# High and low parts of the weight units at addresses that differ from unit to unit, in a hybrid decoder block on one core

## The chip, the core and the metric

The kernel runs on one core of a Trainium2 chip. The metric is the device time of one execution in microseconds. Matrix products are done by TensorE (PE; its loads of the stationary operand are PEld), elementwise work by VectorE (DVE) and ScalarE (ACT), and GpSimd (POOL) and SyncE (SP) mainly start transfers. Each of the 128 partitions of the on-chip memory has its own row of bytes; an address below is a byte offset in that row.

## What is computed

One layer of a decoder block on 256 tokens of width 2048, in fp32. The reference, cut to what matters:

```python
def reference(x, p, w_in, ..., w_gate, w_up, conv_w, conv_b, w_down, ..., w_ple_gate, w_ple_proj):
    mix = token_mixers(x, w_in[i], ..., w_branch_gla[i], w_branch_fox[i], w_out[i])
    x = layer_norm(ALPHA * x + mix, ln1_g[i], ln1_b[i])
    ffn = conv_gated_mlp(x, w_gate[i], w_up[i], conv_w[i], conv_b[i], w_down[i])
    x = layer_norm(ALPHA * x + ffn, ln2_g[i], ln2_b[i])
    x = x + jax.nn.sigmoid(x @ w_ple_gate[i]) * (p[i] @ w_ple_proj[i])

def token_mixers(x, w_in, ...):
    proj = x @ w_in            # q, k, v, gates of two branches, and two merge gates
...
    merged = jax.nn.sigmoid(ma) * y_gla + jax.nn.sigmoid(mb) * y_fox
    return merged @ w_out

def conv_gated_mlp(x, w_gate, w_up, conv_w, conv_b, w_down):
    g = causal_dwconv(x @ w_gate, conv_w, conv_b)
    h = jax.nn.gelu(g) * (x @ w_up)
    return h @ w_down
```

## The kernel before, in words

Nearly all of the work is products of 256 tokens with large weight matrices, in fp32 precision out of a faster matmul format (fp32r). Each operand is split into a high part (its rounding to that format, a copy on ScalarE) and a low part (the operand less its high part, a subtraction on VectorE), and a product is high x high + high x low + low x high.

The weights come as 284 units of 128 x 2048 fp32 (wu, 1 MB each), in one order that the host lays out. unit() hands out the next one and lets prep() run up to three units ahead. prep() loads each half of a unit into a ring of five raw tiles (1024 elements of a partition), makes its high part with copy() (line 121) in a tile of the pool rhi and its low part (line 241) in a tile of the pool rlo. Both pools have six slots. prep_s() does the same for units whose products go by a Strassen scheme; there the block differences are split, in split() (lines 121 and 215).

The units are used in two ways:

- As the stationary operand: w_unit() (lines 307 and 309) and w_phase() (lines 322 and 326), units 0 to 31 (q and k of both branches) and 136 to 223 (gate and up). For each of 16 blocks of 128 input rows one matmul of 512 columns has a 128 x 128 block of the high part as weights (the activation's high and low part stream past it), and one of 256 columns has the same block of the low part.
- As the moving operand: x_mm() (line 353), s_half() (line 841, and 909 in the last half) and q_unit() (line 979), all other units. There 512 columns of a part stream past a 128 x 128 block of the activation.

Where things lie: the built program puts the slots of rhi at 25088, 29184 and so on, 4096 bytes apart, and those of rlo at 49664, 54272 and so on, 4608 apart; all of these are multiples of 256. lo_tile() starts the low part 64 bytes (LO_SHIFT = 16 elements) into its slot where the unit is stationary, and at its start where it is moving (UA lists those units). The activations (xT, x1T, x2T, hC, mS, mC, oT and others) start at multiples of 256, and matmuls use blocks of them at steps of 512 or more. A few tiles lie otherwise: vh, which holds the high part of a head's values for line 1084 as a moving operand, is at 221632, and vl of the first 128 tokens at 225728, both 192 past a multiple of 256 (vl of the other 128 tokens is at 206592 or 208640, multiples of 256). The sums xS of two of the Strassen pairs, stationary in line 841, use the same two places. gp (line 1425) is written from its third element on, 8 bytes past its start; up, of the same shape, from its start.

The order of each engine's instructions is set by the program and the scheduler of the tile framework from what each instruction reads and writes; SP's order is the program's.

Of the kernel before, what the change touches and what calls it, by code (L numbers as in the profile page):

```python
# [10 lines left out]
F32R = mybir.dt.float32r  # L11
# [8 lines left out]
P = 128  # L20
# [15 lines left out]
GAPS = (96, 64, 80)  # L36


LO_SHIFT = 16
UA = (range(32, 136), range(224, 284))  # L40
P_STAT = 5000
P_LN1 = (4000, 2000)
P_LN2 = (4000, 1000)
# [35 lines left out]
def tile_block(ctx: ExitStack, tc: tile.TileContext, wu, wfv, wpp, xT_in, x_in, pT_in, wlr,  # L79
# [11 lines left out]
    rhi = ctx.enter_context(tc.tile_pool(name="rhi", bufs=6))  # L91
    rlo = ctx.enter_context(tc.tile_pool(name="rlo", bufs=6))
# [12 lines left out]
    def s8(shape, dt=F32, name=None):  # L105
        return big.tile(shape, dt, tag="S8", name=name)

    def t1(name):
        return sm.tile([P, 256], F32, tag="t1", bufs=6, name=name)
# [10 lines left out]
    def copy(o, i, scale=1.0):  # L120
        return nc.scalar.activation(o, i, AF.Copy, bias=0.0, scale=scale)  # L121
# [29 lines left out]
    hS = {}  # L151

    def lo_tile(u, name):
        o = 0 if any(u in r for r in UA) else LO_SHIFT
        return rlo.tile([P, 1152], F32R, tag="lo", name=f"lo{name}")[:, o:o + 1024]

    def differences(r0, r1, h, pinned=False):
        b12, b11, b22, b21 = r0[:, 0:512], r0[:, 512:1024], r1[:, 0:512], r1[:, 512:1024]
        sub = lambda o, a, b: nc.vector.tensor_tensor(o, a, b, ALU.subtract)  # L159
        if h == 0:  # L160
            i = sub(b11, b12, b11)
            if pinned:
                tc.keep_in_program_order(i)
            sub(b12, b12, b22)
        else:
            sub(b22, b22, b11)
            sub(b21, b21, b22)
# [17 lines left out]
    def prep_s(u):  # L185


        r0, r1 = [ring.tile([P, 1024], F32, tag="raw", bufs=5, name=f"raw{u}_{h}")
                  for h in range(2)]
        b12, b11, b22, b21 = r0[:, 0:512], r0[:, 512:1024], r1[:, 0:512], r1[:, 512:1024]  # L190
        rt = (r0, r1)
        if u in parked:
            nc.sync.dma_start(b11, wu[u, :, 512:1024])
            nc.sync.dma_start(r1, wu[u, :, 1024:2048])
            w = s8([P, 2048], name=f"td{u}")
            nc.sync.dma_start(w, td[parked[u]])
            rt = (w[:, 0:1024], w[:, 1024:2048])
        else:
            for h, r in enumerate((r0, r1)):
                nc.sync.dma_start(r, wu[u, :, h * 1024:(h + 1) * 1024])  # L200
        if dn0 <= u < dn0 + NF:
            nh = (u - dn0) // (NF // 2)
            pair = DN_ORDER[nh][(u - dn0) % (NF // 2)]
            i = DN_S[0].index(pair)
            if i % 2 == 0:
                two = s8([P, 8, 256], F32R, name=f"hS{nh}_{pair}")
                nc.sync.dma_start(two.bitcast(F32), sd[i // 2].rearrange(
                    "p (i n) -> p i n", i=8))
                hS[nh, pair], hS[nh, DN_S[0][i + 1]] = two[:, 0:4], two[:, 4:8]

        def split(src, name, e=slice(0, 1024)):
            hi = rhi.tile([P, 1024], F32R, tag="hi", name=f"hi{u}_{name}")[:, e]
            lo = lo_tile(u, f"{u}_{name}")[:, e]
            copy(hi, src)
            nc.vector.tensor_tensor(lo, src, hi.bitcast(F32), ALU.subtract)  # L215
            return [(hi[:, o:o + 512], lo[:, o:o + 512]) for o in range(0, src.shape[1], 512)]

        x11, = split(b11, "b11", slice(512, 1024))
        x22, x21 = split(r1, "b2")
        if u not in parked:  # L220
            differences(r0, r1, 0)
        t3, t1_ = split(rt[0], "t13")
        if u not in parked:
            differences(r0, r1, 1)
        t2_, t4 = split(rt[1], "t24")
        ready[u] = [x11, x21, x22, t1_, t3, t2_, t4]

    def prep(pinned=False):
        u = n_prep[0]
        n_prep[0] += 1  # L230
        if u in s_units:
            prep_s(u)
            return
        his, los = [], []
        for h in range(2):
            raw = ring.tile([P, 1024], F32, tag="raw", bufs=5, name=f"raw{u}_{h}")
            nc.sync.dma_start(raw, wu[u, :, h * 1024:(h + 1) * 1024])
            hi = rhi.tile([P, 1024], F32R, tag="hi", name=f"hi{u}_{h}")
            copy(hi, raw)
            lo = lo_tile(u, f"{u}_{h}")  # L240
            i = nc.vector.tensor_tensor(lo, raw, hi.bitcast(F32), ALU.subtract)  # L241
            if pinned:
                tc.keep_in_program_order(i)
            his.append(hi)
            los.append(lo)
        ready[u] = (his, los)


    def unit(ahead=3):
        u = n_used[0]  # L250
        n_used[0] += 1
        while n_prep[0] < min(NU, u + ahead):
            prep()
        return ready.pop(u)
# [203 lines left out]
    for u in range(8):  # L458
        hi, lo = fvu[u]
        for j in range(2):  # L460
# [8 lines left out]
            for t, i, c in seq:  # L469
                o, n = fch[c]  # L470
# [14 lines left out]
        elif u == 4:  # L485
            load_consts()
    prep()
    prep()
    wraw = s8([GROWS, 1024], name="wraw")
    nc.gpsimd.memset(wraw, 0.0)  # L490
# [161 lines left out]
    for n in range(16):  # L652
        h, j = n // 2, n % 2
        hi, lo = unit()
# [114 lines left out]
    for n in range(16):  # L769
        nm, dst, sc = (("q", gq, 1.0 / 16.0), ("k", gk, 1.0))[n // 2 % 2]  # L770
        h, c = n // 4, n % 2
        hi, lo = unit()
# [647 lines left out]
    for n in range(NF):  # L1420
# [18 lines left out]
        u = t1("up")  # L1439
# [4 lines left out]
        if pair in DN_S[0]:  # L1444
            if j == 0:
                yp = t2("yp").rearrange("p (k t) -> p k t", t=S)
            h = yp[:, j, :]
        else:
            h = y
# [4 lines left out]
        if pair in DN_S[0] and j == 1:  # L1454
            v = s_sums(yp)
            for i in range(2):
# [5 lines left out]
                o = k % 2 * 1024 + 512 * i  # L1462
# [295 lines left out]
```

## Time and profile before

| | |
|---|---|
| time, median of 2 runs | 1645.2 us (1645.02 to 1645.38) |
| span of the profiled execution | 1645.0 us |
| granted TensorE clock | 1.000 of full |
| TensorE busy | 1638.4 us (100%), 8422 matmuls |
| weight loads busy | 1404.3 us (85%) |
| VectorE busy | 1356.0 us (82%) |
| ScalarE busy | 910.3 us (55%) |
| moved from and to HBM | 417.53 MB read, 58.73 MB written, 290 GB/s |

The profiled execution took as long as the runs, so its span stands for them. TensorE's matmuls overlap each other in the records: the duration of one (389 ns for 512 columns) is longer than the step from its start to the next one's start, and that step is what adds up to the span. In rows in order of time the first number is a start in us from the span's start, the second the duration. In a group's row the three durations are minimum, median and maximum in ns. In a row by windows stand the window, its length, busy time with the count of instructions, the granted clock, and the DMA engines' share and rate.

### The profile page before, as it was taken

What the parts mean: (1) busy time and instruction counts of PE and PEld (TensorE: products, weight loads), DVE (VectorE), ACT (ScalarE), POOL (GpSimd) and SP (SyncE); (2) the same over time, 40 slices, a digit from 0 to 9 for tenths busy, and PEclk for the clock granted to TensorE, in tenths of its full rate; (3) what the DMA queues carried; (4) which work ended last, traced back from release to release, by engine and by line L of the source; (5) the groups of instructions that cost most, each with busy time, mean ns of one, the idle gap of its engine ahead of it and who ended that gap; (6) DMA issues with size and microseconds to landing.
All of it is one profiled execution on the core that took longest, in us unless ns stands there. A gap on an engine that the chain in (4) does not pass through costs nothing.

```text
span 1645.0 us, 23490 instructions
## 1 busy us (share of the span) xinstructions
PE 1638.4 (100%) x8422; PEld 1404.3 (85%) x8422; DVE 1356.0 (82%) x1964; ACT 910.3 (55%) x1277; POOL 92.7 (6%) x244
## 2 busy tenths in 40 slices
PE   9999999999999999999999999999999999999998
PEld 9988888888888888887898888888888888888887
DVE  7687899788989867778987888887887778988887
ACT  6655555456666654446574445555455456566554
POOL 0000000000000000000010111110111000000000
PEclk9999999999999999999999999999999999999999
DMA  8799799878888768889855898888766679899574
GB/s 324 281 371 341 290 383 356 294 258 309 306 333 307 252 207 303 305 335 364 296 190 194 315 338 320 308 306 304 279 239 217 210 260 336 305 343 348 177 258 157
DMA packets 114838, 477.81 MB, mean 290 GB/s; under 512 B 13032, under 2 KB 14320, under 8 KB 95136
## 3 DMA queue, kind: packets, MB, share of 16 engines
q1 hardware_dynamic: 105216, 417.57, 70.8%
q0 software_dynamic: 9504, 58.73, 8.9%
q8 instruction: 66, 1.08, 0.2%
q14 instruction: 52, 0.43, 0.1%
HBM read 417.53 MB, written 58.73 MB: 290 GB/s over the span
## 4 chain that ended last, share of the span: by engine, by line
PE 97%; DMA 1%; DVE 1%; ACT 0%; issue 0%; POOL 0%; ACTq 0%
PE psm L979 11%; PE dn L841 10%; PE psu L307 10%; PE psg L307 9%; PE psa L979 5%; PE psu L309 5%; PE psg L309 5%; PE dn_p L841 4%; PE gr L841 3%; PE gv L841 3%; PE fv L472 3%; PE pg L353 3%; PE psb L979 3%; PE wo L841 2%; PE gr_p L841 2%; PE gv_p L841 2%
## 5 line engine op out<-in xcount | busy, mean ns | idle before, releaser
L241 DVE TENSOR_TENSOR lo<-raw,hi 128x1024 fp32r<-128x1024 f32 x456 | 551.1, 1220 | 140.7 <-ACT hi L121 139.4
L121 ACT ACTIVATE hi<-raw 128x1024 fp32r<-128x1024 f32 x456 | 476.6, 1057 | 304.2 <-DMA raw<-in_wu_dram 83.7
L307 PE MATMUL psu<-x1T,hi 128*128 128x512 f32 x688 | 240.4, 392 | 0.0
L307 PE MATMUL psg<-x1T,hi 128*128 128x512 f32 x672 | 234.8, 392 | 0.0
L309 PE MATMUL psu<-x1T,lo 128*128 128x256 f32 x688 | 192.3, 280 | 0.0
L309 PE MATMUL psg<-x1T,lo 128*128 128x256 f32 x672 | 187.8, 280 | 0.0
L979 PE MATMUL psm<-hi,xT 128*128 128x512 f32 x512 | 163.0, 392 | 0.0
L307 PEld LDWEIGHTS psu<-x1T,hi 128*128 128x128 f32 x688 | 129.2, 188 | 27.6
L307 PEld LDWEIGHTS psg<-x1T,hi 128*128 128x128 f32 x672 | 126.2, 188 | 27.0
L309 PEld LDWEIGHTS psu<-x1T,lo 128*128 128x128 f32 x688 | 130.6, 190 | 0.0
L121 ACT ACTIVATE hi_b<-raw 128x512 fp32r<-128x512 f32 x112 | 92.9, 841 | 66.8 <-DMA raw<-in_wu_dram 17.9
L309 PEld LDWEIGHTS psg<-x1T,lo 128*128 128x128 f32 x672 | 127.6, 190 | 0.0
L159 DVE TENSOR_TENSOR td<-td 128x512 f32<-128x512 f32 x172 | 117.6, 684 | 0.9
L215 DVE TENSOR_TENSOR lo_b<-raw,hi_b 128x512 fp32r<-128x512 f32 x112 | 104.9, 952 | 15.9 <-ACT hi_b L121 15.6
L979 PEld LDWEIGHTS psm<-hi,xT 128*128 128x128 f32 x512 | 96.2, 188 | 19.6
L215 DVE TENSOR_TENSOR lo_t<-td,hi_t 128x1024 fp32r<-128x1024 f32 x86 | 101.7, 1219 | 12.7 <-ACT hi_t L121 12.0
L121 ACT ACTIVATE hi_t<-td 128x1024 fp32r<-128x1024 f32 x86 | 88.0, 1053 | 28.9 <-DMA td<-td 15.1
L979 PE MATMUL psm<-lo,xT 128*128 128x512 f32 x256 | 99.8, 390 | 0.0
L841 PE MATMUL dn<-hi,hC 128*128 128x512 f32 x352 | 97.8, 389 | 0.0
L979 PE MATMUL psa<-hi,oT 128*128 128x512 f32 x256 | 81.2, 392 | 0.0
L841 PEld LDWEIGHTS dn<-hi,hC 128*128 128x128 f32 x352 | 66.0, 188 | 13.7
L979 PEld LDWEIGHTS psa<-hi,oT 128*128 128x128 f32 x256 | 48.1, 188 | 10.0
(414 smaller groups left out, 3130.8 us busy)
## 6 DMA issues: line engine op xcount, KB each, us to landing
raw<-in_wu_dram SPq DMA_DIRECT2D x525, 512.0 KB, 6.3
td<-in_wu_dram SPq DMA_DIRECT2D x43, 1024.0 KB, 8.8
td<-td POOLq DMA_DIRECT2D x43, 1024.0 KB, 7.7
td<-td SPq DMA_DIRECT2D x43, 1024.0 KB, 8.3
hS<-sd SPq DMA_DIRECT2D x11, 1024.0 KB, 8.8
raw<-in_wu_dram SPq DMA_DIRECT2D x43, 256.0 KB, 7.7
fvraw<-in_wfv_dram SPq DMA_DIRECT2D x13, 524.0 KB, 6.6
sd<-hs POOLq DMA_DIRECT2D x24, 256.0 KB, 5.6
```

Of the source, the lines that this page charges most:

```text
L121: return nc.scalar.activation(o, i, AF.Copy, bias=0.0, scale=scale)
L159: sub = lambda o, a, b: nc.vector.tensor_tensor(o, a, b, ALU.subtract)
L215: nc.vector.tensor_tensor(lo, src, hi.bitcast(F32), ALU.subtract)
L241: i = nc.vector.tensor_tensor(lo, raw, hi.bitcast(F32), ALU.subtract)
L307: nc.tensor.matmul(ps, lhsT=hi[i // 8 if hoff == 0 else 0][:, w0 % 1024:w0 % 1024 + P], rhs=a[:, kt % 4, :], start=first and i == 0, stop= ...
L309: nc.tensor.matmul(ps[:, 256:512], lhsT=lo[i // 8 if hoff == 0 else 0][:, w0 % 1024:w0 % 1024 + P], rhs=a[:, kt % 4, 0:256], start=False, ...
L353: nc.tensor.matmul(bs[j][:, 0:m], lhsT=x, rhs=v[:, o:o + m], start=first and i == 0, stop=last and i == 2)
L472: nc.tensor.matmul(fbk[t][c][:, 0:n], lhsT=x, rhs=w[:, o:o + n], start=kt == 0 and i == 0, stop=kt == 15 and i == 2)
L841: nc.tensor.matmul(ps[:, e], lhsT=x, rhs=w, start=k == 1, stop=k == total.get(id(ps), 3 * ns))
L979: nc.tensor.matmul(ps[t], lhsT=x, rhs=v, start=first and i == 0 and j == 0, stop=last and i == 3 and j == 2)
```

## The change

Both parts now get a place inside a larger slot that depends on the unit's number u: the high part of unit u starts 16 x (u mod 16) bytes into its slot, and its low part 16 x ((5u + u // 16) mod 16) bytes. Both halves of a unit have the same two offsets. Slots of both pools are 1088 elements (4352 bytes = 17 x 256) apart, and since 6 x 4096 + 6 x 4608 = 12 x 4352, no tile outside the two pools moves. The distinction between moving and stationary units (LO_SHIFT, UA) goes. In the built program no instruction is added or removed, and the order of instructions and their waits are the same on every engine.

```diff
-LO_SHIFT = 16
-UA = (range(32, 136), range(224, 284))
...
     def lo_tile(u, name):
-        o = 0 if any(u in r for r in UA) else LO_SHIFT
-        return rlo.tile([P, 1152], F32R, tag="lo", name=f"lo{name}")[:, o:o + 1024]
+        o = 4 * ((5 * u + u // 16) % 16)
+        return rlo.tile([P, 1088], F32R, tag="lo", name=f"lo{name}")[:, o:o + 1024]
+
+    def hi_tile(u, name):
+        o = 4 * (u % 16)
+        return rhi.tile([P, 1088], F32R, tag="hi", name=f"hi{name}")[:, o:o + 1024]
...
         def split(src, name, e=slice(0, 1024)):
-            hi = rhi.tile([P, 1024], F32R, tag="hi", name=f"hi{u}_{name}")[:, e]
+            hi = hi_tile(u, f"{u}_{name}")[:, e]
             lo = lo_tile(u, f"{u}_{name}")[:, e]
...
-            hi = rhi.tile([P, 1024], F32R, tag="hi", name=f"hi{u}_{h}")
+            hi = hi_tile(u, f"{u}_{h}")
             copy(hi, raw)
             lo = lo_tile(u, f"{u}_{h}")
```

## The prediction, as it was made

> **What bounds the kernel now.** I read the page first (busy time, slices, the chain that ended last), then the chain in order of time for stretches that are one kind of matmul only, then the rows of TensorE in order of time wherever an operand lies at an unusual address. From the page:
>
> ```profile
> span 1645.0 us, 23490 instructions
> PE 1638.4 (100%) x8422; PEld 1404.3 (85%) x8422; DVE 1356.0 (82%) x1964; ACT 910.3 (55%) x1277; POOL 92.7 (6%) x244
> PEclk9999999999999999999999999999999999999999
> PE 97%; DMA 1%; DVE 1%; ACT 0%; issue 0%; POOL 0%; ACTq 0%
> ```
>
> The reader is to see that TensorE is never without a matmul and that the chain runs through it for 97% of the time; its clock is not held back in any slice. So the time is a sum of matmuls, and only the start-to-start step of one matmul can move it by much. Two stretches of the chain, and one stage, give that step:
>
> ```profile
> 660.65 10.88 PE psb L979 x48
> 1598.51 10.88 PE pg L841 x48
> 900.00:1300.00 400.00, 400.00 (x2309) 1.00 0.79 285
> ```
>
> 48 matmuls of 512 columns with a weight unit as the moving operand take 10.88 us, 226.7 ns each, in both stretches, 900 us apart and at different lines. The third row is the gate and up stage, where a weight unit is the stationary operand and a 512-column matmul on the high part alternates with a 256-column one on the low part: 400 us for 2309 matmuls is 346.5 ns for a pair. If the columns went at one rate and each matmul had one fixed cost, then from 226.7 for 512 and 346.5 for 512 + 256 the 256-column one costs 119.8, so a column costs 0.418 ns and the fixed part is about 13 ns. That fixed part is the only thing on this path that an address could change.
>
> **The change, part by part.**
>
> *Instructions, order, waits.* None is added, removed or moved: the order and the waits of the built program are the same on all five engines, and the two pools together keep their size (6 x 4096 + 6 x 4608 bytes of a partition before, 12 x 4352 after), so that all tiles behind them keep their addresses. Cost 0. Only the start of a high or low part inside its slot changes: before, each was at a multiple of 256 bytes (low parts in the stages with stationary weights 64 past one), now at a multiple of 16 that depends on the unit, from 0 to 240.
>
> *ScalarE and VectorE, which write the parts.* Here an offset can be seen already:
>
> ```profile
> L336 DVE TENSOR_TENSOR gp<-psg,tmp x44: 411/418/427, 849.9 to 1317.8; 128x256 f32<-128x256 f32 x44
> L336 DVE TENSOR_TENSOR up<-psu,tmp x44: 410/417/425, 853.2 to 1323.3; 128x256 f32<-128x256 f32 x44
> L241 DVE TENSOR_TENSOR lo<-raw,hi 128x1024 fp32r<-128x1024 f32 x456 | 551.1, 1220 | 140.7 <-ACT hi L121 139.4
> ```
>
> The first two do the same work, but gp is written two elements (8 bytes) past its tile's start and up at its start: medians 418 and 417 ns. I take 0 for VectorE, and for ScalarE the same, whose writes of 16-byte offset have no plain row of their own. Were it 10% on VectorE (82% busy), TensorE's lead of two to three units would still cover it in most stages; a price beyond that has no row.
>
> *Weights as the moving operand.* Lines 841, 979 and 353 stream 512 columns of a part:
>
> ```profile
> 0.00:1645.00 1645.00, 504.71 (x2214) 1.00 0.80 290
> 0.00:1645.00 1645.00, 312.26 (x1344) 1.00 0.80 290
> 0.00:1645.00 1645.00, 57.86 (x240) 1.00 0.80 290
> ```
>
> Of the 240 at line 353, 48 (pp<-pw) stream other tiles, so 2214 + 1344 + 192 = 3750 are touched. No part lies off a multiple of 64 before, but one other moving operand lies 192 past a multiple of 256, the tile vh (and vl of one token half; vl of the other half is at a multiple of 256):
>
> ```profile
> 542.67 0.39 PE L1084 MATMUL go<-vh,ath 128*128 128x512 f32 x1
> ...
> 544.07 0.39 PE L1084 MATMUL go<-vh,ath 128*128 128x512 f32 x1
> 544.31 0.39 PE L1084 MATMUL go<-vl,ath 128*128 128x512 f32 x1
> 544.53 0.39 PE L1084 MATMUL go<-vh,atl 128*128 128x512 f32 x1
> 544.76 0.39 PE L979 MATMUL psm<-hi,xT 128*128 128x512 f32 x1
> ...
> 546.38 0.39 PE L979 MATMUL psm<-lo,xT 128*128 128x512 f32 x1
> ```
>
> From 542.67 to 544.07 there are six matmuls, all on operands at 192: 1.40 us, 233.3 ns each. The one at 544.07 is of that kind too (240 in times that are rounded to 10 ns); the one at 544.31 streams the vl that is aligned and takes 220, and its neighbour at 544.53, on vh again, 230. So an address costs, matmul by matmul: about 6.6 ns more than 226.7. Behind them, from 544.76 to 546.38, seven matmuls with all operands at multiples of 256 still take 231.4, 4.7 too many: TensorE needs some matmuls to come back to its short step after a disturbance. One phase of sixteen is thus priced at +6.6; the other fourteen that are not 0 have no row. From below the bound is 0 (nothing seen gets a steady step under 226.7), from above twice 6.6. I take 6.6 for 15 units of 16, since it is the only row of the kind: 3750 x 15/16 = 3516 matmuls, x 6.6 ns = 23.2 us, all on the path.
>
> *Weights as the stationary operand.* Lines 307, 309, 322 and 326 load a part as weights; the stationary tile xS of two pairs also lies at 192 past a multiple of 256, and these rows show it under an aligned moving operand:
>
> ```profile
> 395.45 0.39 PE L841 MATMUL gv<-hi_b,xS 128*128 128x512 f32 x1
> ...
> 398.20 0.39 PE L841 MATMUL gv<-hi_t,xT 128*128 128x512 f32 x1
> 0.00:1645.00 1645.00, 652.28 (x1872) 1.00 0.80 290
> 0.00:1645.00 1645.00, 523.34 (x1872) 1.00 0.80 290
> ```
>
> Twelve matmuls in 2.75 us, 229.2 each: +2.5. The last two rows are lines 307 and 309 (1872 each; 322 and 326 add 144). The low parts are 64 bytes off already before, and still a pair costs 346.5, no more fixed part per matmul than where all is aligned; so for a stationary part the bounds are 0 and +2.5, and 4.7 if the disturbed state lasts. For the low parts, which are off now and later, I take 0; for the 1872 + 96 high parts, aligned until now, 2.5 for 15 of 16: 1845 x 2.5 = 4.6 us. Their weight load runs beside a matmul of only 256 columns, the tighter place, which speaks for the upper of the two values.
>
> *DMA, POOL.* The raw units land in another pool, and neither engine reads a part; 0.
>
> **Sum.** The profiled execution has a span of 1645.0 us, and the two runs are at 1645.02 and 1645.38, median 1645.2: the trace is the run. 1645.2 + 23.2 + 4.6 = 1673.0, 1.7% longer. VectorE and the loads gain slack, as each unit is used up later; TensorE's few waits are too short to give back more than 1 or 2 us.
>
> **The rivals.**
>
> *Nothing happens: 1645.* [...] In the rows' own terms this rival needs vh to be slow for another reason than its address; against it stands the aligned vl in the middle of the same group, at 220. Chance 0.09.
>
> *A gain: about 1628.* The fixed 13 ns would be a collision of stream and weight load, both starting at multiples of 256 all through the kernel, and differing phases would take some of it away. For it speaks only that one aligned step took 220 instead of 226.7; against it, that both rows with unequal phases are slower. If a third of the touched 7638 matmuls (3750 + 3744 + 144) kept such a 6.7 ns, that is 17.1 us: 1628. It decides as soon as the mean step of line 841 falls below 226.7. Chance 0.04; a gain over 2% (33 us, 4.3 ns on each) 0.02 of it.
>
> *Over 2% slower: about 1687.* The state seen from 544.76 on (231.4) needs several matmuls to die away, and with phases that differ between the high and the low part it may never do so; then all 3888 stationary uses pay 4.7 too: 3888 x 4.7 = 18.3 instead of 4.6, 1645.2 + 23.2 + 18.3 = 1686.7. If in addition the 12 phases of 16 that are no multiple of 64 cost a moving operand twice 6.6, 3750 x 0.75 x 6.6 = 18.6 come on top, 1705. For it: no row is known for those 12 phases, and the two known ones were both dearer. Against it: the low parts at 64 cost nothing in 400 us of pairs. Chance 0.39.
>
> **How the numbers follow.** Slower by up to 2% with the moving price as measured, 1655 to 1678: 0.48; nothing 0.09; gain 0.04; dearer 0.39. The forecast is the likeliest case, 1673. Eight times in ten: from 1652 (a quarter of the sum) to 1705, the dear end; outside are no effect and the gain with 0.13, and what is dearer still with 0.07. About 2% of 1645 is 33 us, what a measurement of this kernel is taken to tell from no change; so over 2% faster 0.02, within 2% 0.57 (the likeliest case, no effect and the small gain, with a little cut off at 1678), over 2% slower 0.41.
>
> **What would show it.** TensorE stays at 100% and its clock at full; no wait is new. The stretch at 1598.51 (48 in 10.88) becomes 11.1 to 11.2 where its units are off; units whose number is a multiple of 16 keep 226.7 for their high parts. The window of 400 us in the gate and up stage holds 2294 to 2309 matmuls instead of 2309; fewer than 2280 and the stationary price was too small. Medians of L241 stay at 1218 and of L121 at 1060. I am wrong in the mechanism if the moving stages keep 226.7, and wrong in the size alone if the step is off 233 in the mean, or depends on the unit's phase in another way than 0 against the rest.

## The result, and the profile after

The changed kernel takes 1667.32 us (1667.25 to 1667.38, two runs) where the kernel before takes 1645.2: 1.35% longer, ratio 1.0135 with a 95% interval from 1.0106 to 1.0164. The profiled execution has a span of 1665.6 us against 1645.0. From its page:

```profile
span 1665.6 us, 23490 instructions
PE 1659.5 (100%) x8422; PEld 1402.4 (84%) x8422; DVE 1359.6 (82%) x1964; ACT 912.9 (55%) x1277; POOL 94.1 (6%) x244
PE 99%; DMA 0%; ACT 0%; DVE 0%; SPq 0%; issue 0%; POOL 0%; ACTq 0%; POOLq 0%
L243 DVE TENSOR_TENSOR lo<-raw,hi 128x1024 fp32r<-128x1024 f32 x456 | 552.2, 1221 | 148.0 <-ACT hi L119 147.1
L119 ACT ACTIVATE hi<-raw 128x1024 fp32r<-128x1024 f32 x456 | 477.1, 1058 | 314.2 <-DMA raw<-in_wu_dram 70.2
```

TensorE is still busy for 100% of the span, and its share of the chain went from 97 to 99%. The copy and the subtraction, which write at the new places, cost what they did (1221 ns against 1220 for the subtraction, which is now line 243; 1058 against 1057 for the copy, line 119). So the 20.6 us are steps of matmuls. These are the stretches of 48 matmuls with weights as the moving operand in the chain in order of time, the part that answers to the two stretches of 10.88 us:

```profile
635.34 11.12 PE psb L981 x48
646.46 11.10 PE psa L981 x48
...
738.00 11.20 PE psb L981 x48
...
1618.37 11.06 PE pg L843 x48
```

230.4 to 233.3 ns a matmul, where it was 226.7; the prediction had named 11.1 to 11.2 us for such a stretch. The next rows are windows: the 400 us in the gate and up stage for all of TensorE, then over the whole span the lines 843, 981, 355 (moving) and 309, 311 (stationary), which are 841, 979, 353, 307 and 309 of before.

```profile
900.00:1300.00 400.00, 400.00 (x2292) 1.00 0.79 279
0.00:1700.00 1700.00, 514.77 (x2214) 1.00 0.78 281
0.00:1700.00 1700.00, 318.31 (x1344) 1.00 0.78 281
0.00:1700.00 1700.00, 58.56 (x240) 1.00 0.78 281
0.00:1700.00 1700.00, 656.83 (x1872) 1.00 0.78 281
0.00:1700.00 1700.00, 523.81 (x1872) 1.00 0.78 281
```

A pair of matmuls in the gate and up stage went from 346.5 to 349.0 ns (800 us over 2292); 2292 is two matmuls under the 2294 to 2309 that the prediction named. The moving lines grew by 10.06, 6.05 and 0.70 us, the stationary ones by 4.55 and 0.47. Busy time counts overlaps, so I also added up the steps from each matmul's start to the next start, which have no overlap: line 843 went from 504.77 to 514.03 us, 981 from 307.42 to 313.45, 355 from 55.92 to 56.62, 309 from 432.33 to 436.55 and 311 from 219.40 to 219.74. That is +16.0 us for weights that move and +4.6 for weights that stand, together the 20.6 by which the spans differ.

Sorted by the offset of the moving part, those steps do not separate into 0 and the rest: the mean is 230.5 ns for parts at 0, 230.7 at 64 and at 112, 233.5 at 96, 233.2 at 208, 233.0 at 240, 231.8 over all. Unit 48 has its high parts at 0 and its low parts at 48. Its rows in order of time:

```profile
347.17 0.40 PE L981 MATMUL psm<-lo,xT 128*128 128x512 f32 x1
347.41 0.62 PE L981 MATMUL psm<-hi,xT 128*128 128x512 f32 x2
347.87 0.40 PE L981 MATMUL psm<-lo,xT 128*128 128x512 f32 x1
...
349.28 0.40 PE L981 MATMUL psm<-lo,xT 128*128 128x512 f32 x1
```

Nine matmuls take 2.11 us, 234 ns each. In the trace's unrounded starts the steps of the high parts, whose operands all lie at multiples of 256, are 233 to 235 ns from the third matmul on, and those of the low parts 238 and 239. Unit 256 is the only moving unit with both parts at 0:

```profile
1501.45 1.09 PE L843 MATMUL dn<-hi,hC 128*128 128x512 f32 x4
1502.38 0.62 PE L843 MATMUL dn<-lo,hC 128*128 128x512 f32 x2
1502.83 1.07 PE L843 MATMUL dn<-hi,hC 128*128 128x512 f32 x4
1503.74 0.62 PE L843 MATMUL dn<-lo,hC 128*128 128x512 f32 x2
```

Four matmuls take 0.93 us early in the unit (232 each) and 0.91 later (227): after some matmuls in which nothing is off, the old step is back. That an aligned part among shifted ones pays the same is the first sign against the prediction's mechanism.

### The profile page after: what moved, and what is told of

Read it like the earlier page. It is cut to its first block, busy times and chain, and to the rows that moved or that the text cites. A ratio compares the mean times of both kernels' runs of the same rounds, so it can differ in the third digit from the quotient of the medians.

```text
span 1665.6 us, 23490 instructions
## 1 busy us (share of the span) xinstructions
PE 1659.5 (100%) x8422; PEld 1402.4 (84%) x8422; DVE 1359.6 (82%) x1964; ACT 912.9 (55%) x1277; POOL 94.1 (6%) x244
## 4 chain that ended last, share of the span: by engine, by line
PE 99%; DMA 0%; ACT 0%; DVE 0%; SPq 0%; issue 0%; POOL 0%; ACTq 0%; POOLq 0%
PE psm L981 11%; PE dn L843 10%; PE psu L309 10%; PE psg L309 9%; PE psa L981 5%; PE psu L311 5%; PE psg L311 5%; PE wo L843 4%; PE dn_p L843 4%; PE gr L843 3%; PE gv L843 3%; PE pg L355 3%; PE psb L981 3%; PE fv L474 2%; PE gr_p L843 2%; PE gv_p L843 2%
## 5 line engine op out<-in xcount | busy, mean ns | idle before, releaser
L243 DVE TENSOR_TENSOR lo<-raw,hi 128x1024 fp32r<-128x1024 f32 x456 | 552.2, 1221 | 148.0 <-ACT hi L119 147.1
L119 ACT ACTIVATE hi<-raw 128x1024 fp32r<-128x1024 f32 x456 | 477.1, 1058 | 314.2 <-DMA raw<-in_wu_dram 70.2
L217 DVE TENSOR_TENSOR lo_b<-raw,hi_b 128x512 fp32r<-128x512 f32 x112 | 105.8, 954 | 22.2 <-ACT hi_b L119 21.9
L217 DVE TENSOR_TENSOR lo_t<-td,hi_t 128x1024 fp32r<-128x1024 f32 x86 | 101.7, 1220 | 8.6 <-ACT hi_t L119 8.5
```

## The experiments

Three ideas had to be told apart. In the first, the prediction's, each part pays for its own start: nothing at a multiple of 256, some 6.6 ns elsewhere. In the second, what counts is how the moving and the stationary operand lie to each other. In the third, a row of matmuls runs in a rhythm (a sequence of steps that repeats), the same addresses allow several, and what came before picks one. The quoted expectations name their own theories and price them. All kernels are the changed kernel with other offsets; in the first diff a function place(u) returns the bytes for the high and for the low part of unit u, and the later diffs show only its returns. UA again lists the moving units. The lines are 8 further than in the kernel before (841 is 849, 979 is 987, 307 is 315, 309 is 317).

**moving_only: the change for moving units alone.**

```diff
+    def place(u):
+        if any(u in r for r in UA):
+            return 16 * (u % 16), 16 * ((5 * u + u // 16) % 16)
+        return 0, 64
...
-        o = 4 * ((5 * u + u // 16) % 16)
+        o = place(u)[1] // 4
...
-        o = 4 * (u % 16)
+        o = place(u)[0] // 4
```

> Units 32 to 135 and 224 to 283 (weights as the moving operand) get the changed offsets, the stationary units keep high at 0 and low at 64. Theory A (the step is set by which phases of the high and the low part follow each other in a unit; in the changed kernel's trace it averages 231.9 at every phase, 0 among them): the lines 841, 979 and 353 took 16.0 us more there, so 1661. Theory B (the prediction's: each moving operand off a multiple of 256 costs 6.6 ns by itself): 23.2 more, 1668. Theory C (only a change of phase from one matmul to the next costs, the phase itself nothing): 1661 as well.

Measured: 1662.86 us (1662.81 to 1663.37) against 1645.44 before, ratio 1.0107 [1.0092, 1.0122], so +17.4 us. Line 849, then the gate and up window:

```profile
0.00:1700.00 1700.00, 514.78 (x2214) 1.00 0.78 281
900.00:1300.00 400.00, 400.00 (x2308) 1.00 0.78 281
```

The moving lines have the full growth that they have in the changed kernel, and the gate and up stage has none of it. The first idea's 1668 is not reached.

**stationary_only: the change for stationary units alone.**

```diff
-            return 16 * (u % 16), 16 * ((5 * u + u // 16) % 16)
-        return 0, 64
+            return 0, 0
+        return 16 * (u % 16), 16 * ((5 * u + u // 16) % 16)
```

> Only the stationary units (0 to 31, 136 to 223) get the changed offsets, the moving ones stay at 0. All theories: the remainder, 4.5 us by the lines 307 and 309 of the changed kernel's trace, so about 1650; if the two parts of the change depended on each other, moving_only and this one would not add up to the 22.1 us of the whole change.

Measured: 1649.99 us (1649.21 to 1651.37), 1.0028 [1.0018, 1.0039], +4.5 us. 17.4 and 4.5 make 21.9; the whole change is 22.1. The two parts add up and neither hides the other.

**moving_at_48, moving_at_112, moving_at_192: one phase for all moving parts.** Stationary units stay as before.

```diff
-            return 16 * (u % 16), 16 * ((5 * u + u // 16) % 16)
+            return 48, 48
...
+            return 112, 112
...
+            return 192, 192
```

> High and low parts of all moving units at 48 bytes, the same for every unit; stationary units as before. Theory A, from the one unit of the changed kernel with both parts at 48 (steps 233 and 234 throughout): 3750 x 6.6 = 24.8 more, 1670. Theory B: 1670 too. Theory C: no change of phase inside the moving stages, so 1645.

> The same with 112 bytes in place of 48. Theory A, from the one unit of the changed kernel with both parts at 112 (steps 226 and 227 throughout): 1645. Theory B: 112 is no multiple of 256, or of 64, so 3750 x 6.6 = 24.8 more, 1670. Theory C: 1645.

> High and low parts of all moving units at 192 bytes, the activations (stationary there) at multiples of 256 as before; stationary units as before. After the run with 112 bytes no single unit of the changed kernel is a safe guide, but both vh (233.3, steady) and the unit at 192 (231 and 236 in turn) say 233.5: 3750 x 6.8 = 25.5 more, 1671, if the phase between stream and weight load sets the step; 1645 if only changes of phase cost, which the runs at 48 and 112 speak against.

Measured: 1667.2 us (1.0133 [1.0116, 1.015]) at 48, 1659.6 (1.0087 [1.0072, 1.0102]) at 112, 1667.88 (1.0135 [1.0121, 1.0148]) at 192. At 48 and 192 one constant phase is dearer than the sixteen changing ones of moving_only (1662.86), at 112 a little cheaper. So a change of phase is not needed for a loss, and 112 fits neither of the forecasts for it (1645 and 1670). The chain in order of time, of the kernel at 48 and then of the one at 192:

```profile
670.08 11.20 PE psb L987 x48
```

```profile
670.46 11.20 PE psb L987 x48
```

233.3 ns, which is the price that the tile vh at 192 had shown. At 112 the chain has this:

```profile
610.75 22.19 PE psa L987 x96
...
689.61 5.45 PE psa L987 x24
695.49 5.55 PE psa L987 x24
701.04 11.09 PE psb L987 x48
```

All of these are 512-column matmuls on parts at 112. In the last three rows the 24 of one unit take 227 ns each and the 24 of the next one 231. Single steps in the second are 225, 231 and 238 in turn from its fifth matmul on, in the first 226 or 227 from its second matmul to its last but one. The same offsets thus allow two rhythms, and neither decays into the other within a unit. The row at 610.75 covers four units in 231.1 ns a matmul; its third unit multiplies the same blocks of oT as the unit at 689.61 and, if the six slots are used in turn, lies in the same slots too. The short rhythm is rare here: of the 156 units at lines 849 and 987 three have it, each right behind transposes of another part of the block. A price per phase, which the prediction used, can't give that.

**all_at_192: weights and activations shifted together.** The second entry of GAPS (an unused strip between groups of tiles, in elements) grows by 48, which moves all tiles behind that strip, the activations among them, up by 192 bytes.

```diff
-GAPS = (96, 64, 80)
+GAPS = (96, 64 + 48, 80)
...
+            return 192, 192
+        return 192, 256
```

> All parts of weight units moved by 192 bytes and, by a gap of 192 bytes more ahead of them, all activations too, so that the two operands of each matmul of the big stages stand to each other as before. Theory R (the step depends on how the two operands stand to each other, as they are read side by side): 1645, where moving_at_192 is slow. Theory S (the step depends on the start of the streamed operand alone, as when a line is read that is only partly used): as slow as moving_at_192, 1671 or more, since the stationary operands of gate and up are off too.

Measured: 1645.62 us (1644.77 to 1646.89) against 1645.46, ratio 1.0000 [0.9991, 1.0009]. A stretch of the chain, then the windows of line 849 and of the gate and up stage:

```profile
660.78 10.88 PE psb L987 x48
```

```profile
0.00:1700.00 1700.00, 503.91 (x2214) 1.00 0.77 281
900.00:1300.00 400.00, 400.00 (x2310) 1.00 0.79 285
```

These rows are those of the kernel before to within 1 us, though activations, moving parts and the high parts of stationary units all lie 192 past a multiple of 256 (the low parts of stationary units, 64 past one before, now lie at one). At 192 the moving weights alone cost 22 us; with the activations and the stationary weights moved along, nothing. This is the run that decides between the first idea and the second: for this shift the operand's own start has no price, its place relative to the other operand does. Activations moved alone were not run.

**moving_0_48: high parts aligned, low parts not.**

```diff
+            return 0, 48
```

> Moving units with the high part at 0 and the low part at 48, the same in all units. Theory B (each operand by itself): only the 1250 low parts pay, 8.3 more, 1653.5. Theory A (the pair of phases in a unit): the one unit of the changed kernel with 0 and 48 ran at 235.4, so 3750 x 8.7 = 32.6 more, 1678. A value between says that the rhythm settles in more than one way, as it did at 112.

Measured: 1670.04 us (1669.95 to 1670.52), 1.0148 [1.0132, 1.0163].

```profile
671.76 11.31 PE psb L987 x48
```

235.6 ns, the dearest step of all these stretches, though two of three matmuls stream an aligned part past an aligned activation. By the first idea it had to be cheaper than moving_at_48, and a fixed price for each relative place, the second idea taken alone, fails here too. The order of the matmuls goes along with a difference as well: where two in a row stream the two halves of one part (44 units of line 849), most units have a mean of 232.2.

**stationary_64_0 and stationary_0_0: the two parts of a stationary unit swapped, and both aligned.** Moving units are at 0, as before.

```diff
+        return 64, 0
...
+        return 0, 0
```

> Moving units as before (0, 0); stationary units with the high part at 64 and the low part at 0, the other way round than before. In the changed kernel the three stationary units with the high part at 64 and the low part at 0, 16 and 240 ran at 340.0 ns a pair where before has 346.5: if that is a property of these phases, 1872 x 6.6 = 12.3 less, 1633; if it was the history of these three units, 1645.

> The shift of the low parts of stationary units by 64 bytes taken away, all parts of all units at the start of their slots. The change took this shift away too. In the changed kernel the one unit with both parts at 0 ran at 346.7 a pair, as before's do: 1645 if that is the rhythm that 0 and 0 fall into; up to 10 us more if they mostly fall into a longer one, as 64 and 0 did.

Measured: 1655.01 us (1.0056 [1.0043, 1.0068]) with 64, 0 and 1655.32 (1.006 [1.0046, 1.0074]) with 0, 0, where 0, 64 is the kernel before. The gate and up window of the kernel with 0, 0:

```profile
900.00:1300.00 400.00, 400.00 (x2266) 1.00 0.78 282
```

353 ns a pair against 346.5: with everything at multiples of 256 the stationary stage is slower than with the low parts 64 bytes off, by about 10 us over the kernel. For (64, 0) neither forecast held (1633 and 1645). That kernel shows how a rhythm is lost. Its rows in order of time in the q and k stage, first in unit 9 to 10, then behind the transposes of another part of the block:

```profile
111.52 0.39 PE L315 MATMUL psfk<-xT,hi 128*128 128x512 f32 x1
...
112.88 0.39 PE L315 MATMUL psfq<-xT,hi 128*128 128x512 f32 x1
...
115.56 0.82 PE L602 MATMUL pl<-fqk 128*128 128x128 f32 x4
116.03 0.58 PE L315 MATMUL psfq<-xT,hi 128*128 128x512 f32 x1
116.45 0.28 PE L317 MATMUL psfq<-xT,lo 128*128 128x256 f32 x1
116.57 0.39 PE L315 MATMUL psfq<-xT,hi 128*128 128x512 f32 x1
...
117.62 0.39 PE L315 MATMUL psfq<-xT,hi 128*128 128x512 f32 x1
```

From 111.52 to 112.88 there are four pairs in 1.36 us, 340 ns each, less than any 16 pairs in a row take in the kernel before (346.5 or more). At 116.03 one matmul's step is 0.42 us long, after small matmuls of other kinds; from 116.57 to 117.62 three pairs take 1.05 us, 350 each, and it stays so through the next unit. The offsets are the same on both sides. The late step alone does not say which way it goes: the short rhythm had itself begun at 103.50, behind the same kind of small matmuls, with a step of 0.42 us, out of pairs of 350.

**moving_112_led_in and stationary_led_in: can a unit at another place lead the ones behind it into the short rhythm?** In the changed kernel, units 180 (64, 240), 196 (64, 0) and 212 (64, 16) had run at 340.0 ns a pair in the median, which suggested the places.

```diff
+            return (96, 32) if u % 8 == 6 else (112, 112)
...
+        return (0, 64) if u < 136 else (48, 176) if u % 16 == 3 else (48, 192) if u % 16 == 11 else (64, 0) if 4 <= u % 16 <= 10 else (64, 16)
```

The first line belongs to moving_112_led_in, the second to stationary_led_in; the other kind of unit is as before in both.

> Moving units at 112 and 112 as in moving_at_112 (1659.6), but every eighth (u mod 8 = 6) at 96 and 32, as the unit was that came ahead of the fast one in the changed kernel. Theory H (the step is a rhythm that several repeat themselves at the same addresses, and what came before picks one): units behind such a one run at 226.7 until the next disturbance, so clearly below 1659.6; if all of them did, 1645 plus 22 units x 24 x 6 ns = 3 us, 1649. Theory P (the phases of a unit alone set its step): 1659 to 1660.

> Gate and up units at 64 and 0, or 64 and 16, with one unit in eight at 48 and 176, or 48 and 192, ahead of them, as in the changed kernel ahead of two of its three units of 340.0; q and k units as before (0 and 64). Theory H: 77 of the 88 units at 340.0 instead of 346.6, 77 x 16 x 6.6 = 8.1 us less than before, 1637. Theory P: as in stationary_64_0, whose pairs in this stage ran at 350 and 357 in turn, 1360 x 6.8 = 9.2 more, 1654.

Measured for the moving units: 1660.32 us (1.0088 [1.0074, 1.0102]), the long rhythm 225, 231, 238 as without the lead, so this lead does nothing. For the stationary ones: 1643.4 us (1643.0 to 1644.73), 0.9987 [0.9978, 0.9996]. There the seven units behind each unit at (48, 192) run at 340.0 ns a pair throughout, and those behind each unit at (48, 176) at 350, so the time lies between the two forecasts. The led units differ in place too: the first seven are at (64, 16), the others at (64, 0). So the run doesn't separate the lead from the place. But in the changed kernel unit 196, at (64, 0) behind a unit at (48, 176), took 340, where the same two places give 350 here: that pair of places does not settle the rhythm.

**led_in_once: the lead that works, once.** Unit 139 at (48, 192), all later gate and up units at (64, 16).

```diff
+        return (0, 64) if u < 136 else (48, 192) if u == 139 else (64, 16)
```

> Gate and up units at 64 and 16, with a single unit (number 139, the first whose pairs run without a break) at 48 and 192 ahead of them; all else as before. In stationary_led_in the seven units behind each unit at 48 and 192 ran at 340.0 a pair, at 64 and 16, and did not drift. Theory H (a rhythm keeps itself until something disturbs it; the stage has no wait of TensorE): all 84 units behind it at 340.0 instead of 346.6, 84 x 16 x 6.6 = 8.9 us less than before, 1636.5. If the rhythm is lost on the way, or must be started again every few units: 1640 to 1654.

Measured: 1638.01 us against 1645.6, ratio 0.9966 [0.9953, 0.998], faster than both kernels by more than its interval. The profiled execution:

```profile
span 1635.3 us, 23490 instructions
```

```profile
900.00:1300.00 400.00, 400.00 (x2354) 1.00 0.80 289
```

339.9 ns a pair; the trace's steps are 227 and 113 in all 84 units behind unit 139. At 16 pairs a unit that is 84 x 16 x 6.6 ns = 8.9 us, against 8.5 measured in the profiled execution (1645.6 less 1637.13 us). The twelve runs fall in two groups, seven from 1635.99 to 1638.88 us and five from 1643.49 to 1645.58. The upper group is what the stage without the short rhythm would give, but no execution of that group has a trace, so that its runs lose the rhythm is an argument and not shown. Nor was (64, 16) run without the lead: that the rhythm lasts through 84 units is shown, that unit 139 starts it is not.

## Why the prediction was right in the sum and wrong in the step

*Where the time goes.* Right: TensorE stays full, no wait is new, the loads and the vector work are untouched, and all of the 20.6 us is in the steps of the matmuls on weight units. The forecast of 1673 was 5.7 us too high. That it came so near is in part luck: the price was taken from one offset, and what the sixteen changing ones cost together is seven tenths of it for a reason that the prediction did not have.

*The term that was mis-sized.* "3750 x 15/16 = 3516 matmuls, x 6.6 ns = 23.2 us" measured 16.0 us in the steps of the trace, 17.4 in the run with the moving units alone. Spread over all 3750 that is 4.3 to 4.6 ns each.

*The step that failed under it.* "So an address costs, matmul by matmul": it does not. The price of vh was read rightly, since moving_at_192 gives the same 233.3 ns, but it belonged to a weight at 192 beside activations at 0. all_at_192 takes the price away with the weights still at 192, and moving_0_48 puts 235.6 ns on a mix in which most operands are aligned. Accordingly the sign named for it, "units whose number is a multiple of 16 keep 226.7 for their high parts", did not come (unit 48: 233 and 235), and there is no 1/16 to spare.

*What stood in its place.* In the changed kernel the moving steps have a mean of 231.8 ns, and between 230.5 and 233.5 at every phase. That is near the 231.4 that the prediction had read behind the vh group as a disturbance that needs matmuls to die away; that the two are the same thing is not shown. The rival priced its lasting as an extra for the stationary units; in the runs it lasts in the moving ones, and instead of the 6.6, not on top. In nearly all units of the changed kernel the short step is not come back to; unit 256, with both parts at 0, and unit 71, with both at 112, are where it lasts (steps of 226 and 227 ns).

*The stationary term* came out right, 4.6 forecast and 4.6 measured, in the trace and in stationary_only, for a reason that did not hold: that is luck. It charged the high parts for leaving a multiple of 256. But stationary_0_0, with all parts at such places, is 10 us slower than before, and single units of the changed kernel lie on both sides of the 346.6 ns of before (340.0 for unit 212, 360 for unit 214). The 2.5 ns is a mean over such pairs, and that it met the measured mean is no support for the row that it was taken from.

*The fixed part.* "A column costs 0.418 ns and the fixed part is about 13 ns" was solved from two stages of which only one was in its shortest rhythm. The short one has 226.7 ns for 512 columns and 113.3 for 256, the same 0.443 ns a column, and nothing fixed. The longer steps measured here lie above that; the kernel before has 6.6 ns more in each stationary pair (346.6), which led_in_once takes away (340.0). The rival that expected a gain looked for it in the moving steps and thought that differing phases would find it; it was found in the stationary steps of led_in_once. The aligned step of 220 ns that spoke for that rival came from rounded rows; unrounded it is 226.

*The rival of no effect.* At a chance of 0.09, it needed vh to be slow for another reason than its address. The runs speak against that: moving weights at 192 have the 233.3 ns of vh (moving_at_192, 1.0135), and at 48 the time grows as much (moving_at_48, 1.0133). all_at_192 (1.0000) agrees with the rival only because both operands moved.

*Not settled.* Why a step depends on how the places of the two operands lie to each other, these runs don't show. Nor do they show what picks a unit's rhythm: behind a unit at (48, 192) the units, all at (64, 16), have the short one in every trace; behind (48, 176) units at (64, 0) have it in the changed kernel and not in stationary_led_in; behind (96, 32) it does not come. The place (64, 16) without such a lead stands untested.

## What to carry to other kernels

On a TensorE that is always full, compare start-to-start steps of equal matmuls by stage: when they differ by a few ns while nothing waits (here 226.7 against 231 to 236 for 512 columns), the operands' addresses relative to each other are a cause that can be tried with a few bytes of offset. A uniform price for each operand was the wrong model here: moving weights at 192 cost 22 us beside activations at multiples of 256, and nothing where the activations and the stationary weights were moved along. A constant distance between the two blocks was not enough: of those tried for moving weights only the one of the kernel before (parts and activations both at multiples of 256, or both 192 past one) had 48 matmuls in 10.88 us, 226.7 ns each, while 48 and 192 gave 233.3 and 112 mostly 231, and changing offsets 231.8 in the mean. An offset that happens to be there may matter, as the 64 bytes of LO_SHIFT did (1655.32 us without them against 1645.36), and the fully aligned layout should be measured rather than assumed best.

## What the runs showed of the hardware that was not expected

- With fp32r operands the shortest steps that lasted were 226.7 ns for 512 columns and 113.3 for 256, 0.443 ns a column in both. Longer ones at the same clock were 231 to 236 for 512, and 346.6, 350 or 353 in the mean for a pair of 512 and 256 columns.
- A shift that both operands share cost nothing, a shift of one of them did: with weights and activations moved by 192 bytes the ratio was 1.0000 [0.9991, 1.0009], with the moving weights alone 1.0135 [1.0121, 1.0148].
- Two rhythms each lasted for a whole unit at the same offsets: 5.45 and 5.55 us for 24 matmuls at 112, 340 and 350 ns a pair at (64, 0). In the latter case one gave way to the other behind small matmuls of other kinds, with one late step of 0.42 us, in both directions.
- Aligning everything to 256 bytes was not the fastest for stationary weights: 353 ns a pair, against 346.6 with the low part 64 bytes off, and 340.0 at (64, 16) behind a unit at (48, 192).
